# First-half down-projections of a two-layer encoder: a second sum by transfer, column blocks moved between products, four copies moved to ScalarE

## The chip, the core and the metric

The kernel runs on one core of a Trainium2 chip. The core has TensorE (PE, matrix products into PSUM), VectorE (DVE), ScalarE (ACT), GpSimd (POOL) and SyncE (SP, which here only issues transfers). Each works through its own list of instructions in the order written when the program is built; where one needs another's result, it waits on a semaphore. The metric is the device time of one execution in microseconds.

## The reference

Two encoder layers on 256 tokens of width 2048, all in float32: layer 0 mixes tokens by grouped-query attention, layer 1 by dilated windows, and each is followed by a gated MLP with a width-3 convolution, whose inner width is 5632:

```python
def conv_ffn(h, w_up, conv_w, conv_b, w_down):
    u = h @ w_up
    ...
    u = lax.conv_general_dilated(u, conv_w[:, None, :].astype(u.dtype), ...) + conv_b
    gate, val = jnp.split(u, 2, axis=-1)
    return (jax.nn.silu(gate) * val) @ w_down

def reference(...):
    h = x
    for i in range(DEPTH):
        hn = rms_norm(h, mix_norm[i])
        ...
        h = h + conv_ffn(rms_norm(h, ffn_norm[i]), w_up[i], conv_w[i], conv_b[i], w_down[i])
    return rms_norm(h, final_norm)
```

## The kernel before

**Products.** Every weight is split as it arrives into a high part `wh` (ScalarE, L128) and a rest `wl` (VectorE, L129), and the activations likewise; a float32 product is then three passes of TensorE: high by high, low by high (L318, L320) and high by `wl` (L323). A weight comes in blocks of 128x1024 into one of six buffers `raw` (`new_raw`, `done_raw`: the buffer that was given back first is taken first); a `wh`/`wl` pair comes from a ring of three, in the down-projections four.

**The MLP in halves.** The inner width has 11 pairs of 512-column blocks (gate and value). The first half (`hf` 0) does pairs 0 to 5, the second (`hf` 1) 6 to 10: up-projection, then `up_post` for each block (scale, turn by 32x32 blocks, convolution, SiLU), then the down-projection of that half onto the residual `h`, in two pairs of output columns, (0, 1) and (2, 3). So there are two first halves in the program, one in each layer. In `up_post`, `place_blocks` moves 16 blocks of 32x256 from `t` to `u`; the letters of `PLACE` give the engine of each group of four: "pava" is POOL, ACT, DVE, ACT.

**Seven products for eight.** For chunks 0, 2 and 4 of the first half's six chunks (512 rows of the weight each), `project_pair` does a 2x2 block product in seven products instead of eight. The four weight blocks "11", "21", "12", "22" are summed in their own buffers. A product is a unit of 6 matmuls of 512 columns; a chunk without this trick gives four "usual" units ("c") of 12 matmuls, two for each of the two output columns. The products come in the order `ORDER_D`: 1, 2, 3, 5, 6, 7, 4. With them stand three or four sums of weights (`sums_behind`):

- behind product 1: "11" gets "12" added on VectorE (`add`, L253), then "12" gets the original "22" added by an accumulating transfer from DRAM that POOL issues (`onto`, L249); product 7 needs it.
- behind product 3: "22" gets "11" added on VectorE; products 6 and 4 need it.
- behind product 6: "21" gets "22" added on VectorE, and the buffer of "22" is given back; product 4 needs it.

In the second half the last of these is already an accumulating transfer from one buffer to another, issued behind product 3, and the buffer of "22" is given back at product 6's split (`by_dma=(7, 4)`).

**Order of the units.** `weave` makes the list of units. The first pair of columns (`late`) begins with four usual units, the second with one; the rest of the twelve usual units are spread evenly over the 21 products. In the first pair, in order: products 1, 2, 3, usual, 5, 6, 7, usual, 4; then 1, usual, 2, 3, 5, usual, 6, 7, 4, usual; then 1, 2, usual, 3, 5, 6, usual, 7, 4, usual. Behind the last product the pieces are combined (`combine`, L558 to L570), and `add_residual` (L576) empties the usual units' banks. `tc.high_priority` puts splits and sums ahead of other work in the engines' lists.

**Next stage.** The second half's first up-projection (`seven`, units made in `ffn`) begins with one usual unit, then product 1, then one usual unit behind each of the first five products.

Of the kernel before, what the change touches and what calls it, by code (L numbers as in the profile page):

```python
# [8 lines left out]
F32 = mybir.dt.float32  # L9
# [5 lines left out]
P = 128  # L15
# [4 lines left out]
NPAIR = 11  # L20
NROW = 32 * NPAIR
HALVES = ((0, 6), (6, 11))
# [2 lines left out]
SKG = ((0, 2, 4), (0, 2))  # L25
ORDER = (1, 2, 5, 3, 7, 6, 4)
ORDER_D = (1, 2, 3, 5, 6, 7, 4)
PLACE = "pava"
AHEAD = 45
WOVEN = ((0, 0), (0, 1), (0, 2), (1, 0), (0, 3), (1, 1), (1, 2), (1, 3))  # L30
# [5 lines left out]
def tile_encoder(ctx: ExitStack, tc: tile.TileContext, x, xT, w_a, w_ao, q_gain, k_gain, w_b, w_bo,  # L36
                 rel_bias, gains, w_up, conv, w_down, final_norm, rope, ident_c, onehot, out):
    nc = tc.nc
# [11 lines left out]
    nhalf = cpool.tile([P, 8], F32, name="nhalf")  # L50
    act0 = cpool.tile([P, 8], F32, name="act0")
    nc.gpsimd.memset(nhalf, -0.5)
    nc.scalar.dma_start(gain, gains)
    nc.scalar.activation(act0, nhalf, AF.Copy)
    nc.gpsimd.dma_start(ident, ident_c)
# [157 lines left out]
        return a1  # L213

    def project_pair(w, n0, n1, lhs, forms, units, late, early_done, n0_done, product_done=None, tail=False,
                     lazy=False, by_dma=()):
        home = {1: "M1", 2: "C11", 3: "C12", 4: "C21", 5: "M5", 6: "M6", 7: "M7"}
        if product_done or lazy:
            acc = dict(zip(("C11", "C21", "C12", "C22"), new_acc() + new_acc()))
# [35 lines left out]
        def sums_behind(kg, p):  # L255
            if p == 1:
                add(kg, "11", "12")
                if 7 in by_dma:
                    onto(kg, "12", w[n1, kg][:, 1024:])
                else:  # L260
                    add(kg, "12", "22")
            elif p == 3:
                add(kg, "22", "11")
                if 4 in by_dma:
                    onto(kg, "21", "22")
            elif p == 6 and 4 not in by_dma:
                add(kg, "21", "22")
                done_raw(blocks.pop((kg, "22")))

# [12 lines left out]
        for i, (kind, kg, p) in enumerate(units):  # L282
            if i == late:
                drain()
            if kind == "c":
                r = load_raw(w, (n0, n1)[p // 2], kg, p % 2)
            else:
                b = {1: "11", 2: "21", 3: "22", 5: "11", 7: "12", 6: "22", 4: "21"}[p]
                r = block(kg, b)
            if by_dma:  # L290
                if kind == "P" and p == 1:
                    block(kg, "12")
                if i and units[i - 1][0] == "P":
                    sums_behind(*units[i - 1][1:])
                free = (5, 7, 4) + (6,) * (4 in by_dma)
            else:
                if i + 1 < len(units):
                    prepare(units[i + 1])
                free = (7, 4)
            wh, wl = split_raw(r, kind == "c" or p in free)  # L300
            if kind == "P" and p in free:
                blocks.pop((kg, b))
            todo = []
            if kind == "c":
                for j in range(2):
                    for m, k in enumerate(touched((kind, kg, p))):
                        todo.append((k, *at(lhs[4 * kg + 2 * (p % 2) + j], m), j))
            else:
                f = forms(kg)[p]
                for j in range(2):  # L310
                    x = f[j] if isinstance(f, list) else [t[:, j * P:(j + 1) * P] for t in f]
                    todo.append((home[p], *x, j))
            for k, *_ in todo:
                if k not in acc:
                    acc[k] = bank(4 + ("M1", "M5", "M6", "M7").index(k), "acc") if lazy else ps_tile()
            fresh = {k for k in acc if first[k] == i}
            for k, xh, xl, j in todo:
                nc.tensor.matmul(acc[k], xh, wh[:, j, :], start=k in fresh, stop=False)  # L318
                fresh.discard(k)
                nc.tensor.matmul(acc[k], xl, wh[:, j, :], start=False, stop=False)  # L320
            todo.sort(key=lambda t: (t[0], t[3]))
            for k, xh, xl, j in todo:
                nc.tensor.matmul(acc[k], xh, wl[:, j, :], start=False, stop=last[k] == i and j == 1)  # L323
            if product_done and kind == "P" and home[p][0] == "M":
                product_done(home[p], acc.pop(home[p]))
            if i == last_s:
                early_done(acc)
            if i == max(last["C11"], last["C21"]):
                n0_done(acc)
            if not (product_done or lazy) or kind == "c" or p in (1, 5, 7, 4):  # L330
                step()
# [252 lines left out]
    def ffn(l, hT, ss_in, g_next, last, side=None):  # L584
        with tc.tile_pool(name=nm("wpool"), bufs=1) as wp, tc.tile_pool(name=nm("fpool"), bufs=1) as fp:
# [34 lines left out]
            def up_post(acc, n, cs, after=None):  # L620
                u = us.pop(0)
                us.append(u)
                yield
                s = fp.tile([P, 2, 512], F32, tag="s", name=nm("s"))
                t = fp.tile([P, 2, 512], F32, tag="t", name=nm("t"))
                for m in range(2):
                    nc.scalar.activation(s[:, m], acc[m], AF.Copy, scale=rstd[:, m:m + 1])
                    nc.vector.transpose(t[:, m], s[:, m])  # L628
                yield
                place_blocks(u.rearrange("p j (m t) -> p j m t", m=2), t, PLACE)  # L630
                yield
                for hh in range(2):
                    yield
                    c = cs[hh]
                    for j in range(2):
                        nc.scalar.activation(halves(c[:, j]), halves(u[:, 2 * hh + j])[:, :, :P], AF.Identity,
                                             bias=tap(n, 2 * hh + j, 3), scale=tap(n, 2 * hh + j, 1))
                    for j in range(2):
                        cj, uj = halves(c[:, j]), u[:, 2 * hh + j]
                        nc.vector.scalar_tensor_tensor(cj, halves(uj[:, :NT])[:, ::-1], tap(n, 2 * hh + j, 0), cj,  # L640
                                                       ALU.mult, ALU.add)
                        nc.vector.scalar_tensor_tensor(cj, halves(uj[:, 1:NT + 1])[:, ::-1], tap(n, 2 * hh + j, 2), cj,
                                                       ALU.mult, ALU.add)
                    if after is None:
                        nc.scalar.activation(c, c, AF.Silu)
                    else:
                        yield from after(hh)
# [52 lines left out]
            for hf, (p0, p1) in enumerate(HALVES):  # L700
# [8 lines left out]
                for p in range(p0, p1):  # L709
# [23 lines left out]
                    if hf == 1 and p == p0:  # L733
                        sums = [wp.tile([P, 2, 512], F32, tag=t, name=nm("ms")) for t in ("wh9", "wl9")]
                        c = [("c", k, 2 * n + i) for n in range(2) for k in kgs[1:] for i in range(2)]
                        units = c[:1]
                        for i, f in enumerate(ORDER):
                            units += [("P", 0, f)] + c[1 + i:2 + i] * (i < 5)
                        units += c[6:]
                        cs = []  # L740

                        def gate_ready(a, p=p):
                            cs.extend(new_tiles())
                            start(up_post(a, p, cs[0]))

                        def value_ready(a, p=p, after=after):
                            start(up_post(a, NPAIR + p, cs[1], partial(after, cg=cs[0], cv=cs[1])))

                        seven(w_up[l], p, NPAIR + p, hT, lambda kg: first_forms, units,
                              [[t[:, i] for i in range(2)] for t in sums], gate_ready, value_ready)  # L750
                        continue
# [64 lines left out]
                def weave(lead, late, tail):  # L816
# [3 lines left out]
                    if tail:  # L820
                        c0, c1 = ([u for u in c if u[2] // 2 == n] for n in range(2))
                        c = c0[:-1] + c1[:4] + c0[-1:] + c1[4:-2]
                    units = []
                    units += [c.pop(0) for _ in range(lead)]
                    rest = len(c)
                    for i, u in enumerate(ps):
                        n = min(1, len(c))
                        if hf == 0 or late:
                            n = (i + 1) * rest // len(ps) - i * rest // len(ps)
                        units += [u] + [c.pop(0) for _ in range(n)]  # L830
                    return units + c

# [6 lines left out]
                def first_half(a, n0, n1):  # L839
                    if hf == 1:  # L840
                        finished(n0, n1)
                    done((a["C11"], a["C21"]), n0)

                def pair(n0, n1, late, tail=False):
# [1 line left out]
                    late_at = next(i for i, u in enumerate(units) if u[1] == np_ - 1)  # L846
                    acc = project_pair(wd, n0, n1, slots, forms.get, units, late_at if late else None,
                                       lambda a: start(combine(a, n0, n1, fp, "s", combined)),
                                       lambda a: first_half(a, n0, n1), tail=tail, by_dma=(7, 4) if hf else (7,))
                    accs = acc["C12"], acc["C22"]  # L850
                    if tail:
                        feed(accs, slots, np_ - 1, wd[n1, np_ - 1], False, True, True)
# [572 lines left out]
```

## Time and profile before

| | |
|---|---|
| median of 3 runs | 2234.03 us (2233.73 to 2235.28) |
| the profiled execution | 2236.12 us, span 2234.3 us |
| granted TensorE clock | 0.998 |
| busy: PE, DVE, ACT, POOL | 99%, 83%, 70%, 16% of the span |
| HBM read | 438.11 MB, 199 GB/s over the span |

The profile is one execution, and times in it count from the span's start. A group's line gives the source line, engine, operation, output and inputs, the number of instructions, busy time and mean duration, then the idle time ahead and who ended it. An instruction's recorded duration runs to its last write; the next on the same engine may start before that, so for a queue at work the step from start to start counts. A matmul's recorded end is modelled, so TensorE's pauses are read from the starts as well. In layer 0 the first half's down-projections begin at about 528 us (first pair of columns) and 589 us (second pair), and `seven` at 652 us; in layer 1 the same stages stand 1252.2 us later.

### The profile page before, as it was taken

How to read it: one execution, taken by the hardware profiler on the slowest of the kernel's cores; microseconds unless marked ns; L12 is line 12 of the kernel's file. 1: busy time of each engine (PE TensorE's matmuls, PEld its weight loads, DVE VectorE, ACT ScalarE, POOL GpSimd, SP SyncE). 2: the span in 40 equal slices, each digit the busy share in tenths (PEclk: the TensorE clock that was granted, in tenths of full speed). 3: DMA queues.
4: the chain of work that ended last, by engine and by line, in shares of the span. 5: the costliest groups of instructions: out<-in, count | busy, mean ns of one | idle time of the engine just before them, and what ended most of it. 6: DMA issues, size and time to landing. Idle time of an engine off the chain costs nothing. (4 is left out here: it accounts for less than half of the span.)

```text
span 2234.3 us, 29271 instructions
## 1 busy us (share of the span) xinstructions
PE 2218.5 (99%) x9997; PEld 1835.6 (82%) x9997; DVE 1848.7 (83%) x2543; ACT 1563.9 (70%) x2411; POOL 349.9 (16%) x507
## 2 busy tenths in 40 slices
PE   9999999999999999999999999999999999999998
PEld 7888888888778888888888888888888888888886
DVE  6777778889998888879877988796888899988897
ACT  6665677777557777767876877576777765677764
POOL 2211112211001111111340213010101100001111
PEclk9999999999999999999999999999999999999999
DMA  8444656766766556766655565555665677665675
GB/s 301 160 151 148 202 189 211 233 209 190 234 213 209 194 195 192 244 204 204 217 179 191 170 207 173 189 194 187 195 195 192 205 224 221 208 195 191 222 235 163
DMA packets 129670, 448.99 MB, mean 201 GB/s; under 512 B 17664, under 2 KB 18432, under 8 KB 129520
## 3 DMA queue, kind: packets, MB, share of 16 engines
q1 hardware_dynamic: 119744, 425.64, 57.9%
q0 software_dynamic: 9344, 20.92, 4.9%
q8 instruction: 78, 1.28, 0.2%
q14 instruction: 72, 0.59, 0.1%
q10 hardware_dynamic: 432, 0.56, 0.1%
HBM read 438.11 MB, written 6.29 MB: 199 GB/s over the span
## 5 line engine op out<-in xcount | busy, mean ns | idle before, releaser
L129 DVE TENSOR_TENSOR wl<-raw,wh 128x1024 fp32r<-128x1024 f32 x873 | 1068.6, 1233 | 265.5 <-ACT wh L128 261.5
L128 ACT ACTIVATE wh<-raw 128x1024 fp32r<-128x1024 f32 x873 | 915.6, 1057 | 457.3 <-PE acc L155 162.9
L154 PE MATMUL acc<-wl,xh 128*128 128x512 f32 x1664 | 649.3, 390 | 2.4 <-DVE wl L165 2.1
L153 PE MATMUL acc<-wh,xh 128*128 128x512 f32 x1664 | 649.0, 391 | 0.0
L155 PE MATMUL acc<-wh,xh 128*128 128x512 f32 x1664 | 648.8, 390 | 0.0
L154 PEld LDWEIGHTS acc<-wl,xh 128*128 128x128 f32 x1664 | 313.0, 188 | 68.6 <-DVE wl L165 2.6
L155 PEld LDWEIGHTS acc<-wh,xh 128*128 128x128 f32 x1664 | 312.7, 188 | 64.4
L153 PEld LDWEIGHTS acc<-wh,xh 128*128 128x128 f32 x1664 | 312.8, 188 | 64.0
L318 PE MATMUL acc<-wh,ah 128*128 128x512 f32 x730 | 284.7, 390 | 0.6 <-DVE h L576 0.6
L320 PE MATMUL acc<-wh,al 128*128 128x512 f32 x730 | 284.3, 389 | 0.0
L393 POOL COPY u<-t 32x256 f32<-32x256 f32 x176 | 110.5, 628 | 804.2 <-DVE t L628 796.1
L323 PE MATMUL acc<-wl,ah 128*128 128x512 f32 x730 | 205.2, 390 | 0.5 <-DVE wl L129 0.5
L318 PE MATMUL acc<-wh,xh 128*128 128x512 f32 x416 | 162.8, 391 | 0.0
L320 PE MATMUL acc<-wh,xh 128*128 128x512 f32 x416 | 162.0, 389 | 0.0
L318 PEld LDWEIGHTS acc<-wh,ah 128*128 128x128 f32 x730 | 137.0, 188 | 30.1 <-DVE h L576 1.4
L323 PEld LDWEIGHTS acc<-wl,ah 128*128 128x128 f32 x730 | 136.7, 188 | 30.2 <-DVE wl L129 2.0
L395 ACT ACTIVATE u<-t 32x256 f32<-32x256 f32 x352 | 147.7, 420 | 18.3 <-DVE t L628 10.5
L320 PEld LDWEIGHTS acc<-wh,al 128*128 128x128 f32 x730 | 137.1, 188 | 28.3
L323 PE MATMUL acc<-wl,xh 128*128 128x512 f32 x416 | 113.1, 390 | 0.0
L318 PEld LDWEIGHTS acc<-wh,xh 128*128 128x128 f32 x416 | 78.1, 188 | 16.5 <-DVE h L576 0.4
L323 PEld LDWEIGHTS acc<-wl,xh 128*128 128x128 f32 x416 | 78.0, 188 | 16.2
L320 PEld LDWEIGHTS acc<-wh,xh 128*128 128x128 f32 x416 | 78.1, 188 | 16.0
(270 smaller groups left out, 2486.5 us busy)
## 6 DMA issues: line engine op xcount, KB each, us to landing
raw<-in_w_up_dram SPq DMA_DIRECT2D x352, 512.0 KB, 4.4
raw<-in_w_down_dram SPq DMA_DIRECT2D x176, 512.0 KB, 5.0
raw<-in_w_b_dram SPq DMA_DIRECT2D x144, 512.0 KB, 4.6
raw<-in_w_bo_dram SPq DMA_DIRECT2D x48, 512.0 KB, 4.5
raw<-in_w_a_dram SPq DMA_DIRECT2D x40, 512.0 KB, 4.5
raw<-in_w_ao_dram SPq DMA_DIRECT2D x32, 512.0 KB, 3.8
raw<-in_w_down_dram POOLq DMA_DIRECT2D x17, 512.0 KB, 6.3
raw<-in_w_a_dram SPq DMA_DIRECT2D x16, 256.0 KB, 5.4
```

The lines of the kernel that those rows point to most:

```text
L128: nc.scalar.activation(wh, r, AF.Copy)
L129: nc.vector.tensor_tensor(wl, r, wh.bitcast(F32), ALU.subtract)
L153: nc.tensor.matmul(accs[m], xh, wh[:, j, :], start=st, stop=False)
L154: nc.tensor.matmul(accs[m], xh, wl[:, j, :], start=False, stop=False)
L155: nc.tensor.matmul(accs[m], xl, wh[:, j, :], start=False, stop=sp)
L318: nc.tensor.matmul(acc[k], xh, wh[:, j, :], start=k in fresh, stop=False)
L320: nc.tensor.matmul(acc[k], xl, wh[:, j, :], start=False, stop=False)
L323: nc.tensor.matmul(acc[k], xh, wl[:, j, :], start=False, stop=last[k] == i and j == 1)
L393: nc.gpsimd.tensor_copy(dst, src)
L395: nc.scalar.activation(dst, src, AF.Copy)
```

## The change

1. `by_dma` becomes a table by chunk. In the first half, chunks 0 and 2 take the second transferred sum too: "21" gets "22" by a transfer behind product 3. Chunk 4 keeps it on VectorE. The second half is as before.
2. `weave` for the first half: usual units stand behind products 3 and 6 in the first pair of columns (six of eight, two are left for the end), and behind 3, 5 and 6 in the second (nine of eleven, two left). So between product 7 of one chunk and product 3 of the next stands none.
3. `up_post` of the last pair of each half (pairs 5 and 10, gate and value) uses "paaa": VectorE's four copies go to ScalarE.
4. `seven` begins with two usual units, and has one fewer at its end.
5. A 128x128 tile `ones` is filled by POOL at the start; nothing reads it.

```diff
+BY_DMA = ({0: (7, 4), 2: (7, 4), 4: (7,)}, {0: (7, 4), 2: (7, 4)})
...
+    ones = cpool.tile([P, P], F32, name="ones")
+    nc.gpsimd.memset(ones, 1.0)
...
-                if 7 in by_dma:
+                if 7 in by_dma[kg]:
                     onto(kg, "12", w[n1, kg][:, 1024:])
...
                 add(kg, "22", "11")
-                if 4 in by_dma:
+                if 4 in by_dma[kg]:
                     onto(kg, "21", "22")
-            elif p == 6 and 4 not in by_dma:
+            elif p == 6 and 4 not in by_dma[kg]:
                 add(kg, "21", "22")
                 done_raw(blocks.pop((kg, "22")))
...
-                free = (5, 7, 4) + (6,) * (4 in by_dma)
+                free = (5, 7, 4) + (6,) * (4 in by_dma.get(kg, ()))
...
-                place_blocks(u.rearrange("p j (m t) -> p j m t", m=2), t, PLACE)
+                place_blocks(u.rearrange("p j (m t) -> p j m t", m=2), t, "paaa" if n % NPAIR in (HALVES[0][1] - 1, HALVES[1][1] - 1) else PLACE)
...
-                        units = c[:1]
+                        units = c[:2]
                         for i, f in enumerate(ORDER):
-                            units += [("P", 0, f)] + c[1 + i:2 + i] * (i < 5)
-                        units += c[6:]
+                            units += [("P", 0, f)] + c[2 + i:3 + i] * (i < 5)
+                        units += c[7:]
...
                     for i, u in enumerate(ps):
-                        n = min(1, len(c))
-                        if hf == 0 or late:
+                        if hf == 0:
+                            n = u[2] in ((3, 6) if late else (3, 5, 6))
+                        elif late:
                             n = (i + 1) * rest // len(ps) - i * rest // len(ps)
+                        else:
+                            n = min(1, len(c))
```

Three places of the engines' lists, all in layer 0 (the changed file's lines stand 3 to 5 further down). First ScalarE in the first pair of columns, from the split of the last leading usual unit to that of product 3; `u<-t` are the copies of the last value block, `cv<-u` the convolution that needs all 16 of them. Before:

```order
L128 ACTIVATE wh_5106<-raw_5104 128x1024
L395 ACTIVATE u_2616<-t_5047 32x8x32 x3
L128 ACTIVATE wh_5133<-raw_5129 128x1024
L395 ACTIVATE u_2616<-t_5047 32x8x32 x5
L128 ACTIVATE wh_5151<-raw_5147 128x1024
L636 ACTIVATE cv_4632<-u_2616,cw_2603 128x256 x2
L636 ACTIVATE cv_4633<-u_2616,cw_2603 128x256
L128 ACTIVATE wh_5170<-raw_5168 128x1024
```

After:

```order
L131 ACTIVATE wh_5108<-raw_5106 128x1024
L398 ACTIVATE u_2618<-t_5049 32x8x32 x5
L131 ACTIVATE wh_5135<-raw_5131 128x1024
L398 ACTIVATE u_2618<-t_5049 32x8x32 x7
L131 ACTIVATE wh_5153<-raw_5149 128x1024
L639 ACTIVATE cv_4634<-u_2618,cw_2605 128x256
L131 ACTIVATE wh_5172<-raw_5170 128x1024
```

The splits of products 1, 2 and 3 read raw_5131, raw_5149 and raw_5170 now; twelve copies instead of eight stand ahead of product 2's.

Then VectorE in chunk 2 of the same pair. Before, with product 1 on raw_5262, a usual unit on raw_5276, product 2 on raw_5296 ("21"), product 3 on raw_5308 ("22"):

```order
L129 TENSOR_TENSOR wl_5267<-raw_5262,wh_5266 128x1024
L339 TENSOR_TENSOR al_4627<-cv_4633,ah_4626 128x256
L339 TENSOR_TENSOR al_4629<-cv_4633,ah_4628 128x256
L253 TENSOR_TENSOR raw_5262<-raw_5262,raw_5264 128x1024
L129 TENSOR_TENSOR wl_5281<-raw_5276,wh_5280 128x1024
L129 TENSOR_TENSOR wl_5299<-raw_5296,wh_5298 128x1024
L129 TENSOR_TENSOR wl_5311<-raw_5308,wh_5310 128x1024
L129 TENSOR_TENSOR wl_5322<-raw_5262,wh_5321 128x1024
L253 TENSOR_TENSOR raw_5308<-raw_5308,raw_5262 128x1024
L129 TENSOR_TENSOR wl_5334<-raw_5331,wh_5333 128x1024
L253 TENSOR_TENSOR raw_5296<-raw_5296,raw_5308 128x1024
```

After, with "11" in raw_5264, "21" in raw_5278, "22" in raw_5292, and usual units on raw_5304 and raw_5344:

```order
L132 TENSOR_TENSOR wl_5269<-raw_5264,wh_5268 128x1024
L132 TENSOR_TENSOR wl_5283<-raw_5278,wh_5282 128x1024
L256 TENSOR_TENSOR raw_5264<-raw_5264,raw_5266 128x1024
L132 TENSOR_TENSOR wl_5295<-raw_5292,wh_5294 128x1024
L132 TENSOR_TENSOR wl_5309<-raw_5304,wh_5308 128x1024
L256 TENSOR_TENSOR raw_5292<-raw_5292,raw_5264 128x1024
L132 TENSOR_TENSOR wl_5325<-raw_5264,wh_5324 128x1024
L132 TENSOR_TENSOR wl_5347<-raw_5344,wh_5346 128x1024
L132 TENSOR_TENSOR wl_5335<-raw_5292,wh_5334 128x1024
```

The sum into "21" is gone from VectorE; the usual unit between products 1 and 2 is gone, and the sum into "22" stands behind the split of the usual unit that follows product 3.

Last POOL's list for the two pairs of columns. Before:

```order
L249 DMA raw_5131<-in_w_down_dram 128x1024
L249 DMA raw_5264<-in_w_down_dram 128x1024
L249 DMA raw_5400<-in_w_down_dram 128x1024
L613 MEMSET u_2615 128x4
L249 DMA raw_5584<-in_w_down_dram 128x1024
L613 MEMSET u_2616 128x4
```

After:

```order
L252 DMA raw_5133<-in_w_down_dram 128x1024
L252 DMA raw_5149<-raw_5170 128x1024
L252 DMA raw_5266<-in_w_down_dram 128x1024
L252 DMA raw_5278<-raw_5292 128x1024
L252 DMA raw_5384<-in_w_down_dram 128x1024
L252 DMA raw_5586<-in_w_down_dram 128x1024
L252 DMA raw_5604<-raw_5626 128x1024
L616 MEMSET u_2617 128x4
```

Each of chunks 0 and 2 has a second transfer, from the buffer of "22" to that of "21", behind the first.

More of the change, by code (lines that the diff above doesn't have):

```diff
@@ L215, in project_pair @@
     def project_pair(w, n0, n1, lhs, forms, units, late, early_done, n0_done, product_done=None, tail=False,
-                     lazy=False, by_dma=()):
+                     lazy=False, by_dma=None):
         home = {1: "M1", 2: "C11", 3: "C12", 4: "C21", 5: "M5", 6: "M6", 7: "M7"}
@@ L822, in weave @@
                         c = c0[:-1] + c1[:4] + c0[-1:] + c1[4:-2]
-                    units = []
-                    units += [c.pop(0) for _ in range(lead)]
+                    units = [c.pop(0) for _ in range(lead)]
                     rest = len(c)
                     for i, u in enumerate(ps):
-                        n = min(1, len(c))
-                        if hf == 0 or late:
+                        if hf == 0:
+                            n = u[2] in ((3, 6) if late else (3, 5, 6))
+                        elif late:
                             n = (i + 1) * rest // len(ps) - i * rest // len(ps)
+                        else:
+                            n = min(1, len(c))
                         units += [u] + [c.pop(0) for _ in range(n)]
@@ L848, in pair @@
                                        lambda a: start(combine(a, n0, n1, fp, "s", combined)),
-                                       lambda a: first_half(a, n0, n1), tail=tail, by_dma=(7, 4) if hf else (7,))
+                                       lambda a: first_half(a, n0, n1), tail=tail, by_dma=BY_DMA[hf])
                     accs = acc["C12"], acc["C22"]
```

## Prediction

> **What bounds it now.** I read the page, then the stages at issue by windows, TensorE's waits, and the timeline of each engine there.
>
> ```profile
> PE 2218.5 (99%) x9997; PEld 1835.6 (82%) x9997; DVE 1848.7 (83%) x2543; ACT 1563.9 (70%) x2411; POOL 349.9 (16%) x507
> core 0: us, PE busy (x) PEld busy (x) DVE busy (x) ACT busy (x) POOL busy (x), PEclk, DMA share, GB/s
> 538.64:589.20 50.56, 50.56 (x224) 41.60 (x222) 49.98 (x57) 32.06 (x38) 1.86 (x3) 1.00 0.77 227
> 589.20:651.98 62.78, 62.11 (x271) 50.45 (x270) 57.92 (x60) 34.37 (x35) 2.68 (x4) 1.00 0.78 234
> 651.98:660.88 8.90, 7.39 (x31) 5.48 (x30) 8.50 (x11) 3.50 (x5) 0.00 (x0) 1.00 0.32 112
> 1841.44:1903.83 62.39, 61.95 (x271) 50.31 (x270) 57.88 (x59) 34.37 (x34) 2.69 (x4) 1.00 0.78 234
> PE ps L318 <- DVE cu L569: 1.5, 1, 1.5
> 538.64 0.39 PE L318 MATMUL acc<-wh,ah 128*128 128x512 f32 x1
> 540.00 0.39 PE L318 MATMUL acc<-wh,ah 128*128 128x512 f32 x1
> ```
>
> TensorE is busy all the time, so the change, which keeps every matmul, can win only its pauses. The last two rows are the first matmuls of products 1 and 2: a product of six takes 1.36 us, a usual unit of twelve 2.72. The first pair of columns (from its first product) is 21 products and 8 usual units, 50.3 us, in 50.56: no pause. The second is 21 and 12, 61.2: 1.6 us of pauses in layer 0, 1.2 in layer 1. The start of `seven` (usual, product, usual) is 6.8 in 8.90: 2.1 of pauses, in layer 0 alone, mostly the wait for VectorE's last read of a product's bank (L569). That is 4.9 us to win. And in the first pair VectorE is busy 49.98 of 50.56: it only just keeps ahead.
>
> **Edits with one answer.** The fill of `ones` is a short POOL instruction before anything waits on POOL: nothing. The fewer sums on VectorE by themselves win nothing in the first pair, where TensorE never waits for them. `seven`'s second leading usual unit and the second one left at the end of the pair put 5.4 us between the last product and that bank's next use; the wait was 1.5: the 2.1 us go.
>
> **The first pair of columns.** Steps from start to start come from these rows of VectorE and ScalarE:
>
> ```profile
> 547.31 0.88 DVE L640 SCALAR_TENSOR_TENSOR cv<-u,cw,cv 128x256 f32<-128x256 f32 x2
> 548.10 0.88 DVE L642 SCALAR_TENSOR_TENSOR cv<-u,cw,cv 128x256 f32<-128x256 f32 x2
> 548.90 1.22 DVE L129 TENSOR_TENSOR wl<-raw,wh 128x1024 fp32r<-128x1024 f32 x1
> 550.03 0.69 DVE L650 TENSOR_TENSOR cv<-cg,cv 128x512 f32<-128x512 f32 x1
> 550.63 2.35 DVE L129 TENSOR_TENSOR wl<-raw,wh 128x1024 fp32r<-128x1024 f32 x2
> 553.50 0.76 DVE L339 TENSOR_TENSOR al<-cv,ah 128x256 fp32r<-128x256 f32 x2 [0.51 <-ACT ah L338]
> 554.18 1.22 DVE L253 TENSOR_TENSOR raw<-raw,raw 128x1024 f32<-128x1024 f32 x1
> 555.32 4.63 DVE L129 TENSOR_TENSOR wl<-raw,wh 128x1024 fp32r<-128x1024 f32 x4
> 528.55 1.05 ACT L128 ACTIVATE wh<-raw 128x1024 fp32r<-128x1024 f32 x1
> 529.63 1.31 ACT L395 ACTIVATE u<-t 32x256 f32<-32x256 f32 x3
> 530.96 1.06 ACT L128 ACTIVATE wh<-raw 128x1024 fp32r<-128x1024 f32 x1
> 532.04 2.19 ACT L395 ACTIVATE u<-t 32x256 f32<-32x256 f32 x5
> 534.26 1.06 ACT L128 ACTIVATE wh<-raw 128x1024 fp32r<-128x1024 f32 x1
> 535.23 1.57 ACT L636 ACTIVATE cv<-u,cw 128x256 f32<-128x256 f32 x3
> ```
>
> A split `wl` or a sum steps 1.14, a convolution step (L640, L642) 0.40, a 512-wide one 0.60, an `al` 0.34; a copy on ScalarE 0.44. A product's `wl` is used after four of its six matmuls, 0.91 in, and is recorded 1.22 long: it must start 0.31 before the product does (a usual unit's, 0.6 after).
>
> The copies: twelve instead of eight before product 2's `wh`, so it starts at 536.0, not 534.26, and its `wl` at 537.1. VectorE is spared its four copies but idles for ScalarE's. From there its list to the first product of chunk 2 is nine splits and sums (10.2), four convolution steps and one 512-wide (2.2), two `al` (0.7), again four steps, one 512-wide and two `al` (2.9): 16.0, so that split starts at 553.1. TensorE, whose units before it are as many as now, is there at 553.60: 0.2 us in hand. Now it is done at 551.77 (the second of the pair from 550.63), 1.5 in hand. The sum taken away saves 1.14; the late copies cost more.
>
> Then the block. Now a usual unit follows product 1 of chunk 2; after, products 1, 2, 3 run on, at 553.60, 554.96, 556.32. VectorE has product 2's split, the sum into "11" and product 3's: product 2's at 554.8 (its block loads late, below), product 3's at 557.0. It should start by 556.0: **a pause of 1.0 us**.
>
> Where the two pairs meet, the second usual unit left at the end covers the emptying of the banks, but VectorE has, from the split of chunk 4's product 7 to that of the next product 3, eight splits and sums and eleven 512-wide steps of the combination and the residual: 15.7 against TensorE's 13.6 (four products, three usual units). With 1.7 in hand, by the same count through chunk 4, product 3 waits 0.4, and the usual unit behind it, with one more sum and one more step, 0.7: 1.1 in each layer, against some 1.3 and 1.1 of the pauses now. A gain of 0.2.
>
> **The transferred sum.** One kind stands in the second half already:
>
> ```profile
> raw<-in_w_down_dram SPq DMA_DIRECT2D x176, 512.0 KB, 5.0
> raw<-raw POOLq DMA_DIRECT2D x5, 512.0 KB, 6.7
> 883.91 1.22 DVE L129 TENSOR_TENSOR wl<-raw,wh 128x1024 fp32r<-128x1024 f32 x1
> 885.38 1.22 DVE L253 TENSOR_TENSOR raw<-raw,raw 128x1024 f32<-128x1024 f32 x1
> 887.17 0.86 POOL L249 DMA_DIRECT2D raw<-raw  x1 [7.57 <-DVE raw L253]
> 887.39 0.39 PE L318 MATMUL acc<-wh,ah 128*128 128x512 f32 x1
> 893.82 2.96 ACT L128 ACTIVATE wh<-raw 128x1024 fp32r<-128x1024 f32 x3 [1.32 <-DMA raw<-raw]
> SPq L136 <- DMA raw<-raw: 4.1, 1, 4.1
> ```
>
> The sum into "22" starts at 885.38, POOL issues 1.79 later, it lands 6.7 after that. Two then wait: ScalarE's split of product 4, with all ScalarE's list behind it, and SP, which stands 4.1 us because the next chunk's "21" loads into the buffer of "22", with every later load queued behind. There TensorE never noticed: four usual units stand in a chunk, and product 3 was split at 883.91, over 3 us ahead of its start at 887.39. That lead also hides ScalarE's four more copies a block in the second half: nothing, and up to 1 us for each of the two blocks of a layer if it were gone.
>
> In the first half's first pair only two do. Chain it from the start of product 3's `wl` in chunk 2: that split and the usual unit's, which the list puts first (2.3), sum to issue (1.8), landing (6.7), load of chunk 4's "21" (5.0), `wh` to `wl` and use (1.1 and 0.3): 17.2, or 16.9 from product 3's start on TensorE. TensorE's own work to chunk 4's product 2 is 6 products and 2 usual units, 13.6: **a pause of 3.3 us**, some of it already at product 4, whose split waits for the same landing. From chunk 0 to chunk 2 the same chain starts 2.7 us ahead of TensorE with the sum first, and costs the 0.1 that is in the figures above. In the second pair of columns three usual units make TensorE's part 16.3, and the chain, where the sum follows at once or one step later, 15.7 to 16.3: no pause.
>
> [...]
>
> **The sum.** Two layers of 1.0 + 3.3 = 8.6, less 2.1 and 0.2: 6.3 slower. On the profiled execution's 2236.1 that is 2242.4; it stands 2.1 above the median of the runs shown, and on that, 2234.0, the forecast is 2240.3. 0.2% is 4.5 us, about what a measurement of this kernel can tell from no change.
>
> **Rivals.** First, the transfers are quick enough: not slower.
>
> ```profile
> DMA to landing us min/median/max: 4.5/6.4/7.6
> DMA to landing us min/median/max: 3.7/5.0/7.2
> 900.21 0.87 POOL L249 DMA_DIRECT2D raw<-in_w_down_dram  x1 [12.18 <-DVE raw L253]
> 906.76 0.87 POOL L249 DMA_DIRECT2D raw<-raw  x1 [5.69 <-DVE raw L253]
> ```
>
> The first row is all POOL's transfers onto blocks, the second SP's loads in the first half's down-projections of layer 0. At their short ends the chain is 16.9 - 2.2 - 1.3 = 13.4, under 13.6: it decides from 3.3 us less. Then 2.0 lost, 2.3 won: 2233.7; with the 2.0 not lost and 1.2 more won at the seam of the pairs, 2230.5. For it: such landings occur. Against: the raw<-raw ones have a median of 6.7. Chance 0.28. [...]
>
> Second, VectorE, with two sums fewer in each pair, runs ahead and every pause goes: 2234.0 - 4.9 = 2229.1, faster. Needed is a lead of 3.3 us at product 3 of chunk 2; I count 1.0 behind. Chance 0.12.
>
> Third, worse: in chunk 2 the two transfers would be issued 3.4 us apart, in the rows above 6.55. If the second waits for the first to land, it is 3.3 later in each layer: 6.6 more, 2246.9. Chance 0.08.
>
> **Numbers.** The forecast has 0.52; with landings around the medians its loss runs from 3.5 to 9, and it is over 4.5 in 0.43 of the 0.52. The first rival lies within 0.2%, the second is faster in 0.10, the third slower: slower 0.51, same 0.39, faster 0.10. The range leaves out the second rival and the third: from the far end of the first, 2230.5, to a forecast with both landings 1.5 us longer in one layer, 2243.3.
>
> **What would show it.** Right: in the first pair of columns TensorE pauses at product 3 of chunk 2 and again at product 4 or at product 2 of chunk 4, about 4 us together, in both layers; SP's waits on raw<-raw grow from 4.1 us once to one for each chunk; ScalarE waits on raw<-raw in the first halves; `seven` in layer 0 starts without its 1.5 us wait. Wrong: the first pair still takes 50.6 us, or TensorE's waits there name something other than `wl` or a late `wh`.

## The result, and the profile after

2255.7 us is the median of four executions. One of them, 2457.99, ran at a granted clock of 0.85 and is left out of all that follows; the others took 2254.22, 2254.35 and 2257.06, median 2254.35. Before has 2234.66 on the same chip. The ratio is 1.0092, 95% interval 1.0072 to 1.0112: slower by some 20 us, where 6.3 were forecast and the range ended 9.3 above the 2234.0 that it was worked out from. The profiled execution of after took 2257.06, its span is 2255.3; the two traces differ by 21.0.

The page's groups of TensorE (busy and mean, then idle ahead and its releaser):

```profile
L157 PE MATMUL acc<-wl,xh 128*128 128x512 f32 x1664 | 649.5, 390 | 4.3 <-DVE wl L132 2.4
L321 PE MATMUL acc<-wh,ah 128*128 128x512 f32 x730 | 287.2, 393 | 9.5 <-ACT wh L131 9.4
L326 PE MATMUL acc<-wl,ah 128*128 128x512 f32 x730 | 207.8, 394 | 1.5 <-DVE wl L132 1.4
```

and of before, the group that is L321 above:

```profile
L318 PE MATMUL acc<-wh,ah 128*128 128x512 f32 x730 | 284.7, 390 | 0.6 <-DVE h L576 0.6
```

The waits for `wh` (L321, the first matmuls of a product or usual unit) are new; before, TensorE's largest single wait behind the first 10 us was for VectorE, 1.5. The stages of after by windows, from the first matmul of each to that of the next (of a second pair, from its second): ahead of layer 0's first half, its two pairs of columns, `seven`, the stretch around the second half's first products, and layer 1's two pairs:

```profile
core 0: us, PE busy (x) PEld busy (x) DVE busy (x) ACT busy (x) POOL busy (x), PEclk, DMA share, GB/s
500.38:539.78 39.40, 38.83 (x171) 31.84 (x170) 30.45 (x45) 33.21 (x56) 5.90 (x9) 1.00 0.59 189
539.78:595.96 56.18, 53.55 (x225) 42.62 (x223) 50.62 (x60) 33.74 (x40) 3.45 (x4) 0.97 0.79 233
595.96:663.81 67.85, 64.00 (x270) 51.24 (x269) 54.83 (x57) 33.43 (x36) 4.54 (x7) 0.97 0.77 225
663.81:712.34 48.53, 48.17 (x212) 39.45 (x210) 42.22 (x53) 31.24 (x42) 2.49 (x4) 1.00 0.60 194
870.54:957.10 86.56, 85.59 (x376) 70.25 (x375) 75.80 (x97) 64.84 (x101) 10.80 (x16) 1.00 0.72 222
1803.65:1859.75 56.10, 53.42 (x224) 42.69 (x223) 50.58 (x60) 33.84 (x40) 3.45 (x4) 0.97 0.79 235
1859.75:1923.87 64.12, 62.28 (x270) 50.07 (x269) 54.06 (x56) 33.28 (x36) 4.52 (x7) 1.00 0.81 233
```

Cut at the same matmuls, counted from the start of the program, the trace of before has 38.53, 50.78, 62.56, 50.11, 85.00, 50.64 and 62.33 here. Three of the seven rows have a granted clock of 0.97; before had 1.00.

The first pair of layer 0, chunk 2: POOL's two accumulating transfers, ScalarE's splits, and the landing of the second transfer:

```profile
558.23 0.86 POOL L252 DMA_DIRECT2D raw<-in_w_down_dram  x1 [14.25 <-DVE raw L256]
561.63 0.86 POOL L252 DMA_DIRECT2D raw<-raw  x1 [2.54 <-DVE raw L256]
DMA to landing us min/median/max: 8.8/8.8/8.8
563.78 1.06 ACT L131 ACTIVATE wh<-raw 128x1024 fp32r<-128x1024 f32 x1 [1.60 <-PE acc L326]
570.53 1.06 ACT L131 ACTIVATE wh<-raw 128x1024 fp32r<-128x1024 f32 x1 [5.69 <-DMA raw<-raw]
```

The second is issued 3.4 after the first and lands at 570.4; ScalarE, which takes its list in order, stands 5.69 for it. TensorE there (starts; a whole step at full clock is 0.23), and the same place by windows:

```profile
568.76 0.61 PE L326 MATMUL acc<-wl,ah 128*128 128x512 f32 x2
571.64 0.50 PE L321 MATMUL acc<-wh,ah 128*128 128x512 f32 x1 [2.26 <-ACT wh L131]
...
573.92 0.63 PE L321 MATMUL acc<-wh,ah 128*128 128x512 f32 x1
574.35 0.63 PE L323 MATMUL acc<-wh,al 128*128 128x512 f32 x1
574.77 0.63 PE L321 MATMUL acc<-wh,ah 128*128 128x512 f32 x1
```

```profile
568.90:571.60 2.70, 0.48 (x3) 0.05 (x1) 0.00 (x0) 1.07 (x2) 0.00 (x0) 1.00 0.44 155
572.80:576.20 3.40, 3.34 (x9) 2.62 (x9) 3.40 (x7) 2.37 (x4) 0.00 (x0) 0.50 0.95 367
624.00:627.40 3.40, 3.40 (x9) 2.62 (x10) 3.37 (x3) 3.40 (x4) 0.49 (x1) 0.50 0.18 36
1835.80:1839.10 3.30, 3.30 (x9) 2.56 (x8) 3.30 (x6) 1.90 (x3) 0.00 (x0) 0.50 0.96 364
```

So a pause of 2.4 at product 4, and 1.2 behind it the granted clock falls to 0.50 for 3.4 us: matmuls step 0.43 instead of 0.23. Layer 1's first pair does the same (a step of 2.60 at 1832.85, then the last row). The third such stretch is in layer 0's second pair, where the pause is longer. POOL, ScalarE and TensorE there, with the landings of the transfer from 604.60 and of SP's loads issued at 613.25 and 614.42:

```profile
604.60 0.86 POOL L252 DMA_DIRECT2D raw<-raw  x1 [5.84 <-DVE raw L256]
DMA to landing us min/median/max: 8.2/8.2/8.2
612.86 2.01 ACT L131 ACTIVATE wh<-raw 128x1024 fp32r<-128x1024 f32 x2 [1.84 <-DMA raw<-raw]
SPq L139 <- DMA raw<-raw: 4.4, 1, 4.4
DMA to landing us min/median/max: 7.3/7.8/8.3
617.40 1.06 ACT L131 ACTIVATE wh<-raw 128x1024 fp32r<-128x1024 f32 x1 [2.53 <-DMA raw<-in_w_down_dram]
622.78 2.00 ACT L131 ACTIVATE wh<-raw 128x1024 fp32r<-128x1024 f32 x2 [4.32 <-DMA raw<-in_w_down_dram]
623.89 0.72 PE L321 MATMUL acc<-wh,ah 128*128 128x512 f32 x1 [3.38 <-ACT wh L131]
```

Here ScalarE waits 1.84 for the transfer itself, without a pause of TensorE. SP waits for it too, because its next load goes into the buffer of "22": it stands 4.4 us, then issues four loads in 2.4 us. With another accumulating transfer behind them these take 4.5, 7.3, 8.3 and 9.4, and a split waits 4.32 for the last but one. That they come in a burst is not shown to be what slows them: the two loads before SP stood, issued 1.1 apart at 606.05 and 607.18, took 7.7 and 8.8.

### The profile page after: what moved, and what is told of

It reads as the page before. It is cut to its first block, busy times and chain, and to the rows that moved or that the text cites. A ratio compares the mean times of both kernels' runs of the same rounds, so it can differ in the third digit from the quotient of the medians.

```text
span 2255.3 us, 29301 instructions
## 1 busy us (share of the span) xinstructions
PE 2228.1 (99%) x9997; PEld 1838.4 (82%) x9997; DVE 1824.1 (81%) x2503; ACT 1574.1 (70%) x2443; POOL 355.8 (16%) x516
## 5 line engine op out<-in xcount | busy, mean ns | idle before, releaser
L321 PE MATMUL acc<-wh,ah 128*128 128x512 f32 x730 | 287.2, 393 | 9.5 <-ACT wh L131 9.4
L326 PE MATMUL acc<-wl,ah 128*128 128x512 f32 x730 | 207.8, 394 | 1.5 <-DVE wl L132 1.4
L398 ACT ACTIVATE u<-t 32x256 f32<-32x256 f32 x384 | 161.0, 419 | 17.9 <-DVE t L631 9.4
L321 PEld LDWEIGHTS acc<-wh,ah 128*128 128x128 f32 x730 | 138.3, 189 | 41.2 <-ACT wh L131 12.0
L326 PEld LDWEIGHTS acc<-wl,ah 128*128 128x128 f32 x730 | 137.0, 189 | 34.1 <-DVE wl L132 6.2
L321 PE MATMUL acc<-wh,xh 128*128 128x512 f32 x416 | 162.7, 391 | 0.0
L326 PE MATMUL acc<-wl,xh 128*128 128x512 f32 x416 | 113.1, 390 | 0.0
L326 PEld LDWEIGHTS acc<-wl,xh 128*128 128x128 f32 x416 | 78.0, 188 | 16.2
L321 PEld LDWEIGHTS acc<-wh,xh 128*128 128x128 f32 x416 | 78.1, 188 | 16.0
```

Of the source, the lines that this page charges most:

```text
L398: nc.scalar.activation(dst, src, AF.Copy)
```

## The experiments

All are compared with before on the same chip. Stages are cut as above, at the same matmuls; a cell is the difference to the trace of before, layer 0 / layer 1, and "2nd half" is layer 0's stretch from 860 to 945. The stage ahead of 500 us, which nothing here touches, differs by up to 2.7 from that of before and is not in the table.

| kernel | median, over before | ahead | first pair | second pair | `seven` | 2nd half |
|---|---|---|---|---|---|---|
| changed | +19.7 | 0.9 / 0.9 | 5.4 / 5.5 | 5.3 / 1.8 | -1.6 / 0.7 | 1.6 |
| e1 no transfer | +10.4 | 0.9 / 0.9 | 2.3 / 2.8 | 0.5 / 1.4 | -1.6 / 0.7 | 2.8 |
| e2 copies back | +7.4 | 0 / 0 | 2.6 / 2.0 | 2.2 / 2.5 | -1.6 / 0.7 | 0 |
| e3 even units | +24.2 | 0.9 / 0.9 | 9.0 / 7.5 | 2.4 / 2.3 | -0.6 / 1.7 | 1.0 |
| e4 transfer alone | +16.6 | 0 / 0 | 4.8 / 3.2 | 1.8 / 2.7 | 2.6 / 1.1 | 0.1 |
| e5 chunk 0 alone | +7.3 | 0.9 / 0.9 | 1.7 / 1.2 | 0.9 / 1.0 | -1.6 / 0.7 | 2.6 |
| e6 buffer later | +27.9 | 0.9 / 0.9 | 8.3 / 6.2 | 7.3 / 2.2 | -1.6 / 0.7 | 4.0 |
| e7 copies alone | +15.9 | 0.9 / 0.9 | 5.1 / 4.5 | 0.5 / 1.1 | 2.0 / 0.3 | 1.1 |
| e8 units and seven | +2.0 | 0 / 0 | 1.0 / 1.0 | 0.1 / 1.0 | -1.6 / 0.7 | 0 |
| e9 one transfer | +14.2 | 0.9 / 0.9 | 5.1 / 4.5 | 0.6 / 0.7 | -1.6 / 0.7 | 2.3 |
| e11 copies, old transfer out | +15.8 | 0.9 / 1.2 | 3.1 / 3.7 | 0.9 / 2.7 | 0 / 0.6 | 2.0 |
| c1 seven, layer 0 | -1.0 | 0 / 0 | -0.1 / 0.1 | -0.4 / 0.3 | -1.3 / 0 | 0 |
| c2 c1 and chunk 0 | +4.5 | 0 / 0 | -0.1 / 1.5 | 3.7 / 2.8 | -1.6 / 0 | 0.4 |
| c3 c2, changed order | +1.4 | 0 / 0 | 0.9 / 0.3 | 0.7 / 0.8 | -1.6 / 0 | 0.7 |

**Undoing one part of the change.** e1 takes the transfer out, e2 the copies:

```diff
-BY_DMA = ({0: (7, 4), 2: (7, 4), 4: (7,)}, {0: (7, 4), 2: (7, 4)})
+BY_DMA = ({0: (7,), 2: (7,), 4: (7,)}, {0: (7, 4), 2: (7, 4)})
```

> The changed kernel, with its second sum back on VectorE in all chunks of the first half; copies, order of units and start of seven as changed. Theory (late landings of the second transferred sum, and the half clock behind their pauses, carry about 16 of the 21 us): the pauses behind wh at product 4 and at the next chunk's product 2 go, and the half clock with them; the copies' 4.4 stay: 2239 to 2241. Rival A (the usual units standing between products 3 and 7 make VectorE late, transfer or not): VectorE has 1.14 more for each of two chunks and pair, so the pauses stay and name wl: 2250 to 2258. Rival B (the copies on ScalarE carry most): 2250 or more.

```diff
-place_blocks(..., t, "paaa" if n % NPAIR in (...) else PLACE)
+place_blocks(..., t, PLACE)
```

> The changed kernel, with the last blocks' copies shared with VectorE again; transfer, order and start of seven as changed. Theory: the feed matmuls' waits for wl (eight pauses, 4.4 us together) go, the first pairs lose 0.5 each, the late landings stay: 2250 to 2252. Rival B (the copies carry most, by making ScalarE late for product 4's split too): 2240 or less. Rival C (the copies cost nothing, those waits have another cause): 2255 to 2256.

e1: 2245.59, ratio 1.0046 (1.0031 to 1.0061); e2: 2242.65, ratio 1.0033 (1.0020 to 1.0046). Both miss, e2 by much: without the copies 12 us go, nearly three times the 4.4 that was put down to them; but e1, which keeps them, is 9 faster too, so neither part carries the loss by itself. The table says why: in a first pair the copies or the transfers alone, on top of e8, cost 1.0 to 1.7, both together 4.4 and 4.5. In neither is there a pause over 0.6 in a first pair, nor a stretch at half clock in any stage (granted clock over the profiled execution 0.999 in both, 0.996 in the changed kernel).

e3 spreads the usual units of the first half evenly, as before, and keeps the rest; e4 is before with the transfers alone (`BY_DMA` as changed):

> The changed kernel, with its usual units spread evenly over the first half's pairs as before; transfer, copies and start of seven as changed. Theory: in the first pair one usual unit fewer stands between products 3 and 4 of chunk 2, so product 4 waits up to 2.7 longer for the same landing, in each layer, while the second pairs change little: 2257 to 2262. Rival A (the placing of the units makes VectorE late): most of the loss goes, 2240 to 2246.

> The kernel before, with the second transferred sum alone (evenly spread units, copies shared, start of seven as before). Theory: pauses of 3 to 6 us at product 4 of chunk 2 or at the next product 2 in each pair, with half clock behind those over 2.5 us: 2248 to 2258, some 16 above before. Rival A: under 2240, since the units stand as before. Rival B: under 2240, since the copies are as before.

e3: 2259.41, ratio 1.0109 (1.0092 to 1.0126); e4: 2251.82, ratio 1.0075 (1.0060 to 1.0090). Both times are as the theory had them, the stages only in part: in e3 layer 0's second pair, which was to change little, gets back 2.9 of its 5.3, and in e4 the longest pauses of the four pairs are 3.5, 1.4, 2.4 and 1.5, where 3 to 6 were expected. The 2.5 us that e4's theory gives for half clock was the author's estimate: in the changed kernel half clock followed steps from matmul to matmul of 2.60, 2.65 and 3.78, in e4 one of 2.46 and not one of 2.63. The order of the units is a help to the transfer, not the cost: rival A falls, and e8 (below) seals it. In e3 TensorE's steps at product 4 of chunk 2 are 4.83 and 5.03.

**Which transfer.** e5 keeps the second transferred sum in chunk 0 alone, `{0: (7, 4), 2: (7,), 4: (7,)}`:

> The changed kernel with the second transferred sum in chunk 0 alone; chunk 2 sums on VectorE. Theory (each pause behind wh hangs on the landing of one transfer): the pauses of 2.4 in both layers' first pairs hang on chunk 2's transfer and go with their half clock, the 3.6 of layer 0's second pair hangs on chunk 0's (SP stood until it had landed) and stays: 2255.7 - 4.0 x 2 = 2247 to 2249. Rival (chunk 2's two transfers, 3.4 apart, hinder one another and chunk 0's are innocent): no pause behind wh over 1 us in any pair, 2244 to 2246.

2241.56, ratio 1.0034 (1.0021 to 1.0047): better than either. Chunk 0's transfer is innocent here: with it the first pairs are 0.7 and 1.6 shorter than with none (e1); the sum that VectorE is spared would explain it, which was not tested. Chunk 2's costs 12.4. That layer 0's second pair would keep its pause was wrong: with the first pair in time, chunk 0's transfer there landed after 6.7, not 8.2.

e9 leaves chunk 2 its second transferred sum and puts the first, "12", back on VectorE, behind product 2:

```diff
+BY_DMA = ({0: (7, 4), 2: (4,), 4: (7,)}, {0: (7, 4), 2: (7, 4)})
...
-                else:
-                    add(kg, "12", "22")
+            elif p == 2 and 7 not in by_dma[kg]:
+                block(kg, "22")
+                add(kg, "12", "22")
```

> The changed kernel with chunk 2's first transferred sum (into 12, from memory) put back on VectorE, behind product 2; its second one (into 21) stays a transfer. Theory 'in one another's way' (chunk 2's second transfer took 8.8 and 8.7 in the first pairs, others 6.5 to 7.3, since the first was under way until 2.0 after its issue): it lands in 6.5 to 7, and the pauses behind it fall from 2.4 to under 1.5, without half clock, though VectorE has 1.14 more: 2249 to 2252. Rival (the landing is long because SP's loads run beside it; what counts is VectorE's lateness): it takes 8 or more again, or is issued over 1 later: 2255 to 2260.

2249.15, ratio 1.0066 (1.0052 to 1.0080). POOL's transfer, its landing, and TensorE's waits in layer 0's first pair:

```profile
560.72 0.86 POOL L252 DMA_DIRECT2D raw<-raw  x1 [19.42 <-DVE raw L256]
DMA to landing us min/median/max: 6.7/6.7/6.7
PE acc L327 <- DVE wl L132: 1.4, 3, 0.6
PE acc L322 <- ACT wh L131: 0.9, 2, 0.8
```

(L327 and L322 are the changed kernel's L326 and L321 here.) With SP's loads as near as in the changed kernel (one 1.6 ahead, two up to 1.8 behind) but no other accumulating transfer on its way, it lands in 6.7, 2.1 sooner; in the changed kernel the first of the two was under way until 2.0 after the second's issue. The long wait and the half clock are gone (granted clock 1.00 from 537.09 to 592.95). The overlap alone does not make a landing long, though: the changed kernel's transfer at 1886.99, in layer 1's second pair, began while another had 2.3 to go, with no load of SP on its way, and landed in 6.7. The first pair gains only 0.3 and 1.0, because VectorE pays 1.14 for the sum and several waits for `wl` take the place; the second pairs gain 4.7 and 1.1.

e6 gives back the buffer of "22" one release later, so that SP might load elsewhere meanwhile (`hold` is set at product 6's split where its sum is transferred, in the second halves too):

```diff
-        free_raw.append(raw_tag.pop(id(t))[0])
+        i = raw_tag.pop(id(t))[0]
+        if hold:
+            held_raw.append(i)
+            return
+        free_raw.append(i)
+        while held_raw:
+            free_raw.append(held_raw.pop())
```

> The changed kernel with the buffer of block 22, after its transferred sum, handed out one release later, so that SP's next load goes to another buffer and does not stand behind the transfer's landing. Theory, part SP (held loads that then come in a burst make the second pair's pause): layer 0's second pair falls from 5.3 to under 2 above before, SP's waits on raw<-raw fall from 46 to under 25, the first pairs' 2.4 pauses (ScalarE's split of product 4 waiting itself) stay: 2251 to 2253. Rival (the landing itself is waited for everywhere, SP's standing costs nothing): 2255 to 2257.

2262.2, ratio 1.0126 (1.0111 to 1.0141): slower still, and SP's waits on raw<-raw stayed, 46.8 against 46.2. The next load then waits for the next buffer instead, and comes no sooner. So it does not tell the two theories apart; a seventh buffer, which might, was not tried.

**One part alone.** e7 is before with the copies on ScalarE, e8 before with the order of units and the start of `seven`:

> The kernel before with the last blocks' copies on ScalarE, nothing else. Theory (ScalarE alone has the twelve copies, so the feed matmuls wait for wh and wl): some 3 to 5 us in the stages ahead of the down-projections, as in the run without transfers (0.9 ahead of each first half, 2.7 before layer 0's second half), and up to 1 in each first pair: 2238 to 2241. Rival (copies cost only through VectorE's being late for the transfer): 2234 to 2236.

> The kernel before with the new places of the usual units and the new start of seven; no second transfer, copies shared. Theory (seven's start in layer 0 gains 1.6, in layer 1 it loses 0.7; the units bunched cost VectorE's lead little): 2233 to 2236. Rival A (the placing of the units is itself a cost of several us): 2238 or more.

e8: 2236.24, ratio 1.0008 (0.9999 to 1.0017), 0.2 over the theory's range and under rival A's. e7: 2250.13, ratio 1.0071 (1.0054 to 1.0088), nine more than the theory allowed. ScalarE and POOL in chunk 2 of layer 0's first pair, before:

```profile
555.97 0.89 POOL L249 DMA_DIRECT2D raw<-in_w_down_dram  x1 [19.54 <-DVE raw L253]
563.37 2.01 ACT L128 ACTIVATE wh<-raw 128x1024 fp32r<-128x1024 f32 x2 [1.11 <-DMA raw<-in_w_down_dram]
```

and in e7, with a matmul behind:

```profile
557.53 0.88 POOL L252 DMA_DIRECT2D raw<-in_w_down_dram  x1 [21.27 <-DVE raw L256]
564.93 2.95 ACT L131 ACTIVATE wh<-raw 128x1024 fp32r<-128x1024 f32 x3 [5.16 <-DMA raw<-in_w_down_dram]
566.98 0.50 PE L321 MATMUL acc<-wh,ah 128*128 128x512 f32 x1 [1.96 <-ACT wh L131]
...
569.42 0.63 PE L323 MATMUL acc<-wh,al 128*128 128x512 f32 x1
```

The transfer into "12" was in the kernel before, and ScalarE waited for it there (7.3 from issue to landing) without TensorE's noticing. In e7 POOL can issue it only 1.56 later, 2.3 counted from the pair's first product (537.94 against 538.64), since VectorE's sum ahead of it is late by the copies; the slack is gone, product 7 pauses 2.1, and half a clock follows (0.50 from 568.60 to 571.90).

e10 and e11 are one kernel: e7 with that transfer put back on VectorE in chunk 2 (`{0: (7,), 2: (), 4: (7,)}` and the edit of e9). The trace is e11's.

> The kernel before with the copies on ScalarE, as in the run of the copies alone, and chunk 2's transferred sum into 12 put back on VectorE, behind product 2. Theory (the copies alone cost 4.5 to 5.1 in each first pair because VectorE, 1.1 late, issues this transfer 1.6 later and ScalarE's list stands at its landing, 2.3 and half a clock behind it): the 2.3 pause behind wh goes with its half clock, VectorE's 1.14 more shows as pauses behind wl of 1 to 2 together: first pairs 2 to 3 above before, 2243 to 2246. Rival (the first pair loses because VectorE's list as such is too long): first pairs 5 or more above before, 2250 or more.

> The same kernel as the copies alone with chunk 2's transferred sum into 12 on VectorE, again, for its profile. Theory (landing): first pairs 2 to 3 above before, pauses behind wl only, no half clock there; the time above 2250 would then have to come from the second pairs or the start of seven. Rival (VectorE's list itself, with one sum of 1.14 more in each pair): first pairs 4 or more above before.

e10: 2249.93, ratio 1.0071 (1.0055 to 1.0087), 4 more than its theory allowed; e11: 2249.86, ratio 1.0070 (1.0056 to 1.0084). TensorE's listed waits in layer 0's first pair are now

```profile
PE acc L327 <- DVE wl L132: 1.6, 2, 1.4
```

The pause for `wh` and the half clock of the first pair are gone, as the landing theory has it, but the gain is 2.0 and 0.7, with 2.0 more in layer 0's `seven`; the second pairs and the second half lose 2.9, and between the medians of e7 and e11 only 0.3 is left. This reads as VectorE's 1.14 more for each pair of columns coming out later, and as the copies costing by two ways, through the landing and through VectorE's list; it was not tested further.

**In search of a better version.** c1 is before with two leading units for `seven` in layer 0 alone (`c[:2 - l]`); c2 adds chunk 0's second transferred sum; c3 adds to c2 the changed order of units.

> The kernel before with seven's two leading usual units in layer 0 alone. By the stages of the runs so far (seven's start 1.6 shorter in layer 0, 0.7 longer in layer 1, where before has no pause): 1.6 faster, 0 to 2.1: 2232 to 2234. If the gain needs the second usual unit left at the end of the pair of columns, none: 2234 to 2235.

> The same with the second transferred sum in chunk 0 of the first halves. Theory (with four usual units ahead chunk 0's landing is covered, and VectorE has 1.14 less in each pair): the pauses where the pairs meet, 1.3 and 1.1 before, shrink by up to 1.1 each, so 1.6 to 3.8 faster than before: 2230.5 to 2232.7. Rival (any second transferred sum in a first half costs): 2236 or more.

> The kernel before with the changed order of usual units, seven's two leading units in layer 0, the second transferred sum in chunk 0 alone, copies shared as before. Theory (with two usual units between products 3 and 4 a landing of 6.7 is covered, and VectorE has 1.14 less in each pair): first pairs 0 to 0.5 above before, second pairs 0 to 1, seven 1.6 under: 2233 to 2235, no difference that can be measured. Rival (the sum in chunk 0 costs its 2 to 4 us in the second pairs, whatever the order): 2237 or more.

c1: 2233.99, ratio 0.9996 (0.9987 to 1.0005); c2: 2239.51, ratio 1.0025 (1.0015 to 1.0034); c3: 2235.51, ratio 1.0004 (0.9995 to 1.0013). The stages show c1's 1.3 in `seven`, but no version is shown to beat before. c3 is 0.5 over its theory's range. c2 came out as its rival had it, and fails in the second pairs:

```profile
601.95 0.87 POOL L252 DMA_DIRECT2D raw<-raw  x1 [9.34 <-DVE raw L256]
DMA to landing us min/median/max: 9.1/9.1/9.1
611.20 2.01 ACT L131 ACTIVATE wh<-raw 128x1024 fp32r<-128x1024 f32 x2 [8.06 <-DMA raw<-raw]
612.30 0.50 PE L321 MATMUL acc<-wh,ah 128*128 128x512 f32 x1 [2.88 <-ACT wh L131]
612.64 0.39 PE L323 MATMUL acc<-wh,al 128*128 128x512 f32 x1
```

In the even order fewer usual units stand between products 3 and 4, and this one took 9.1 with no other accumulating transfer near; SP issued loads 0.8 ahead of it and 0.3 behind. Why these loads slow it and those of e9 don't was not settled. In all the traces together, each of the ten transfers from buffer to buffer that began 0.5 to 0.8 behind a load of SP took 7.8 to 9.1 (four in e3, four in e4, two in c2), where 11 of the 125 others took 7.8 or more; no run tests this as a cause.

## Why the prediction was wrong

- **The first pair of columns**: 4.3 forecast for each layer, 5.4 and 5.5 measured. Both pauses stand where they were put: at product 3 of chunk 2, 0.6 instead of 1.0, waiting for `wl`; and behind the transferred sum, 2.4 at product 4 instead of 3.3 spread up to the next product 2. Two things were mis-sized. The landing was 8.8, not 6.7: the third rival's mechanism, two transfers in one another's way, which had a chance of 0.08 and which e9 bears out at this place, 2.1 for its 3.3, though the overlap alone is not enough (1886.99, above). And the half clock behind the pause, 1.2 to 1.4 over whole matmuls, was no term at all. It also covered the next load: TensorE came so late to chunk 4's product 2 that it waited for nothing there in layer 0 and 0.4, for `wl`, in layer 1. So the 4.3 came within 1.2 partly by errors that cancel. The signs named for the first pair did come, and SP's waits on raw<-raw grew from 13.1 us in 3 to 46.2 in 11: the mechanism there was right, its sizes were not.
- **The second pair**: the step that failed. "No pause" was taken from a chain of 15.7 to 16.3 against 16.3, both ends made with median landings of 6.7 and 5.0. Measured in layer 0 are 8.2 for the transfer, and 7.3 and 8.3 for loads that SP issued behind it. The second pairs cost 5.3 and 1.8 (a pause of 3.6 and half clock in layer 0, two waits of 0.9 for `wh` in layer 1) against a forecast gain of 0.2 in all. e1, without the transfer, has 0.5 and 1.4 there. What made these landings long stays open: e6 could not tell.
- **The copies ahead of the down-projections**: forecast nothing; 0.9 ahead of each first half, from both sides (there in every kernel with the copies, gone in every one without), and some 0.5 at 877 in layer 0's second half. The lead of 3 us that was to hide them was read at product 3 of a later chunk; at the feeds themselves nothing stood in hand. A further 1.0 at 940 was not shown to be theirs: that place costs 0 to 3.2 from kernel to kernel, 0.6 in c3, which has no such copies.
- **The copies in the first pair**: 1.0 was their whole price. Alone they cost 5.1 and 4.5 (e7), because the old transfer into "12" had no slack either. It was in the trace of before, ScalarE waiting 1.11 for it, and was not looked at.
- **`seven`**: the 1.5 us wait is gone and 1.6 of the 2.1 came in layer 0; a usual unit fewer at its end makes a feed behind it wait 0.5. In layer 1, which had nothing to win, that is a loss of 0.7; in c1, c2 and c3, where layer 1 keeps its order, it is 0.

Summed over the table, before rounding: 1.7 + 10.9 + 7.1 - 0.9 + 1.6 = 20.4 of the 21.0 between the traces, 4.0 of it matmuls at half clock (six and twice seven of them, 0.2 each). The first rival's ground, transfers of 4.5, was there in one landing of thirteen.

## What to carry to other kernels

Where a list in order waits for a transfer, price the landing at its worst neighbour, not at its median: here 8.7 and 8.8 with another accumulating transfer 3.4 ahead, and 7.8 to 9.1 begun 0.5 to 0.8 behind a load of SP, against a median of 6.7. And ask first which waits of the same kind already stand there without slack. Two edits that each eat the same slack don't add up: here the copies and the transfers cost 1 to 2 us each on top of e8 in a first pair, and 4.5 together. Of TensorE's pauses of over 2 us that are listed below most were followed by half clock and four were not, so a forecast with such a pause should carry a surcharge for it, 1.2 to 1.4 us in the changed kernel.

## What the runs showed of the hardware

**The clock after short pauses.** The granted clock fell to 0.50 behind pauses whose step from matmul to matmul was 2.34 (e7), 2.41 (e6), 2.46 (e4), 2.54 (e7), 2.60 and 2.65 (changed), and behind all of 3.70 and more; for 3.41 us each, and for twice that behind the longest, 4.83 and 5.03 (e3) and 5.82 (e6). It stayed at 1.00 behind 2.57 (e7), 2.63 (e4), 3.26 (c2, rows above) and 3.47 (e6). So in these traces the length of a step alone does not tell which of them half clock followed. In the changed kernel, behind the first 20 us and ahead of the last 12, the clock changes at 572.79, 576.21, 623.99, 627.41, 1835.72 and 1839.14, whole multiples of 3.413 us apart, with 1, 14, 1, 354 and 1 of them between; in the trace of before it changes at 8.43, 11.84 and 2230.50, with 1 and 650 between. Cut the traces into stretches on that grid and add up TensorE's idle time in each, from 0.23 behind the start of a matmul to the start of the next, leaving out the same 20 and 12 us. In the changed kernel the three full-clock stretches just ahead of the half clock have 2.49, 3.31 and 2.41 idle, and no other has over 1.06; in before, which has no half clock there, none has over 1.03. Counted over the traces of all these kernels, the eleven full-clock stretches with 2.26 or more idle were followed by half clock, and of those with 1.96 or less none was. The step of 2.60 fell into one stretch, the one with 2.41; e6's 3.47 was shared by two, with 1.41 and 1.94.

**Landings.** Of the changed kernel's thirteen accumulating transfers from buffer to buffer, 512 KB each, nine took 6.5 to 7.3 and one 4.5. The two issued 3.4 behind another accumulating transfer took 8.7 and 8.8, the one that began layer 0's second-pair loss 8.2, with the other one 6.7 ahead of it. In e2, where the other was 4.3 and 4.4 ahead, it was 6.9 and 6.7.
